# Dilated attention: reload and merge weights emitted four steps later, PSUM banks in three shared pools

## The chip, the cores and the metric

The kernel runs on one core of a Trainium2 chip. Its time is the device time in microseconds, the median of several executions. Beside the times there is a trace of one profiled execution.

## The reference

The kernel computes two transformer blocks on 2048 tokens of width 1024, in float32. The change lies in the first block's dilated attention: 8 heads of 64 columns, and three patterns (window, dilation), which are merged by their softmax denominators:

```python
DIL_PATTERNS = ((128, 1), (512, 4), (2048, 16))
# dilated_branch: query t attends to t + j*dilation, |j| <= window // (2*dilation)
    s = einsum('bnqche,bnkche->bnchqk', qs, kw) * scale + bias   # bias = -slope * distance
    s = where(mask, s, MASK_VALUE)
    m = max(s, axis=-1, keepdims=True); e = exp(s - m); l = sum(e, axis=-1, keepdims=True)
    o = einsum('bnchqk,bnkche->bnqche', e, vw) * (1.0 / l)
    lse = m + log(l)
# dilated_attention
    w = softmax(stack(lses, axis=0), axis=0)
    out = sum(w[..., None] * stack(outs, axis=0), axis=0)
# block
    y = concatenate([a, b], axis=-1) * silu(z);  x = x + y @ w_out
```

## The kernel before

The kernel is one program in six stages, one after the other: projections, differential attention, dilated attention (`phase_b2`, 1321 to about 1709 us of the span), the output product with its gate, and two stages of the second block. Matmuls take their float32 operands as a high and a low part.

`phase_b2` splits the patterns in two. The dense part (names with `n`: d_sn, d_en, d_tn, d_nh, d_nl) is the pattern of dilation 1, with the tokens in their order. The residue part (names with `r` or none: d_sr, d_er, d_tr, d_ph, d_pl) takes the four residue classes mod 4 and holds the patterns of dilation 4 and 16 in one score matrix. Each part has, per head, 16 blocks of 128 queries. For a block, TensorE makes scores into PSUM (L564, L591); VectorE adds the bias and takes the row minimum of the negated scores (L567, L594); ScalarE makes the exponentials with their row sum (L570, L596); TensorE transposes them (L604 into d_tn, L623 into d_tr); they are copied out of PSUM in two parts (dense: ScalarE d_pn, L607, then GpSimd d_nh and d_nl, L611 and L612; residue: ScalarE d_ph, L625, VectorE d_pl, L626); TensorE multiplies them with the values into d_or (L638, L734), four blocks at a time; ScalarE copies that to d_ta (L644), TensorE transposes it back into d_ob (L650), and VectorE sums it into d_o1 or d_o2 (L651).

The dense result of a head (d_o1, with its minimum and sum in two more columns) is in another order of tokens than the residue result (d_o2). So it is stored to DRAM (s_o, L657) and loaded back in the order of the residue classes (d_a, L661, in `load_merge`). Both DMAs are issued on ScalarE's queue; the load waits for the store to land. `load_merge` also loads the gate sz (L665) on SyncE. `weights` (L676) computes the two merge weights: nine small VectorE operations from L686 (d_mm, the first to read d_a) to L696, with two exponentials on ScalarE. The merge itself (scale both results, add, multiply by sz, store to s_y: L702, L719, L720, L673) is on GpSimd and stands in a list `later`, of which one piece is emitted per step (two after the last scores).

The loop goes over steps n: 16 steps are a head, scores of step n are those of the dense blocks n and n + 1 (at even n) and of the residue block n - 3; the other operations follow some steps behind. Counted from a head's first step, its dense result is complete and stored at step 21, `load_merge` is emitted at step 24, `weights` at step 27, the last `back_res` at step 27 too, and the merge's pieces at steps 27 to 35. Head h begins at step 16h. The loads of head h + 1 (q and k, then vn, then vr) are emitted on SyncE at steps 4, 6 and 11 of head h, with the scaled biases of that head (L526, L527) on ScalarE at step 4.

What is emitted is not what each engine runs in order. The program is built with `schedule_with_timeline_sim=True`: a planner with its own model of durations places each instruction on its engine when its inputs and its buffer are free in that model; among instructions that are ready, the one emitted first goes first. The order it makes is fixed in the program, and an engine runs it in that order: an instruction that waits holds up all behind it. The PSUM pools of the stage take eight banks in all, one for a tile; a pool with the same tag for several names hands its banks to whichever comes.

Of the kernel before, what the change touches and what calls it, by code (L numbers as in the profile page):

```python
# [7 lines left out]
F32 = mybir.dt.float32  # L8
# [5 lines left out]
PSUM = bass.MemoryType.PSUM  # L14
DRAM = bass.MemoryType.DRAM

P = 128
# [446 lines left out]
LB = 4  # L464
# [1 line left out]
LEAD = 3  # L466
DN = 2
DR = 2
BACK = 3
WT = 8  # L470


def phase_b2(tc, c, scr, nat_bias, res_bias, res_two):
    nc = tc.nc
    NS = 8 * NT
    with (
# [6 lines left out]
        tc.tile_pool(name="d_h1", bufs=1) as hp1,  # L483
        tc.tile_pool(name="d_p", bufs=2) as pp,
        tc.tile_pool(name="d_o", bufs=2) as op,
        tc.tile_pool(name="d_pon", bufs=1, space=PSUM) as po_n,
        tc.tile_pool(name="d_por", bufs=1, space=PSUM) as po_r,
        tc.tile_pool(name="d_ptr", bufs=2, space=PSUM) as pt_r,
        tc.tile_pool(name="d_psn", bufs=1, space=PSUM) as ps_n,
        tc.tile_pool(name="d_psr", bufs=2, space=PSUM) as ps_r,  # L490
        tc.tile_pool(name="d_ptn", bufs=1, space=PSUM) as pt_n,
    ):
        nb0 = bp.tile([P, 256], F32, name="d_nb0")
        nc.sync.dma_start(nb0, nat_bias)
# [58 lines left out]
        def scores_nat(n):  # L553
            h, t = divmod(n, NT)
            q, k, _, _ = hd[h]
            if t == 0:
                o1s[h] = op1.tile([P, NT, 66], F32, name="d_o1")
                o2s[h] = op.tile([P, NT, 64], F32, name="d_o2", tag="d_o2")
            ml = o1s[h][:, t:t + 2, 64:66]
            ps = ps_n.tile([P, 2, 256], F32, name="d_sn")  # L560
            en = tp.tile([P, 2, 256], F32, name="d_en", bufs=3)
            for u in range(2):
                for i in range(2):
                    nc.tensor.matmul(ps[:, u], q[:, (t + u) * P:(t + u + 1) * P],  # L564
                                     k[i][:, (t + u) * P:(t + u) * P + 256], start=i == 0, stop=i == 1)
            for u in range(2):
                nc.vector.tensor_tensor_reduce(en[:, u], ps[:, u], nb[h % 2], 1.0, 3.0e38, ALU.add, ALU.min,  # L567
                                               ml[:, u, 0:1])
            for u in range(2):
                nc.scalar.activation(en[:, u], en[:, u], AF.Exp, bias=ml[:, u, 0:1], scale=-1.0,  # L570
                                     accum_out=ml[:, u, 1:2])
            en_[n] = en
# [5 lines left out]
        def scores_res(n):  # L578
            h, t = divmod(n, NT)
            q, k, _, _ = hd[h]  # L580
            if t == 0:
                m2s[h] = [sp.tile([P, NT], F32, name=nm, bufs=2) for nm in ("d_m2", "d_l2")]
            g4, s0 = divmod(t, 4)
            cls = 4 * s0 + g4
            m2, l2 = m2s[h][0][:, cls:cls + 1], m2s[h][1][:, cls:cls + 1]
            qr = q.rearrange("p (j r g) -> p j g r", r=P, g=4)[:, s0, g4]
            ps = ps_r.tile([P, 512], F32, name="d_sr")
            lo, hi = span(s0)
            for i in range(2):
                kr = k[i][:, 64:S + 64].rearrange("p (b g u) -> p g b u", g=4, u=16)[:, g4, lo // 16:hi // 16]  # L590
                nc.tensor.matmul(ps[:, lo:hi], qr, kr, start=i == 0, stop=i == 1)  # L591
            er = tp.tile([P, 512], F32, name="d_er")
            off = (3 - s0) * P
            nc.vector.tensor_tensor_reduce(er[:, lo:hi], ps[:, lo:hi], rb[h % 2][:, off + lo:off + hi], 1.0,  # L594
                                           3.0e38, ALU.add, ALU.min, m2)
            nc.scalar.activation(er[:, lo:hi], er[:, lo:hi], AF.Exp, bias=m2, scale=-1.0, accum_out=l2)  # L596
            er_[n] = er

        def trans_nat(n):
            en = en_.pop(n)  # L600
            pt = pt_n.tile([P, 2, 2, P], F32, name="d_tn")
            for u in range(2):
                for j in range(2):
                    nc.tensor.transpose(pt[:, u, j], en[:, u, j * P:(j + 1) * P], c["id"])  # L604
            t = n % 4
            pn = up.tile([P, 2, 2, P], F32, name="d_pn")
            nc.scalar.activation(pn, pt, AF.Copy)  # L607
            if t == 0:
                pn_[n // 4] = [pp.tile([P, 4, 2, P], F32R, name=nm) for nm in ("d_nh", "d_nl")]
            nh, nl = pn_[n // 4]  # L610
            nc.gpsimd.tensor_scalar(nh[:, t:t + 2], pn, 1.0, 1.0, ALU.mult, ALU.mult)  # L611
            nc.gpsimd.tensor_sub(nl[:, t:t + 2], pn, nh[:, t:t + 2].bitcast(F32))  # L612

        def trans_res(n):
            h, t = divmod(n, NT)
            er = er_.pop(n)
            g4, s0 = divmod(t, 4)
            if s0 == 0:
                rpt[h, g4] = (pp.tile([P, 4, 4, P], F32R, name="d_ph"), pp.tile([P, 4, 4, P], F32R, name="d_pl"))
            pt = pt_r.tile([P, 4, P], F32, name="d_tr")  # L620
            ka, kb = [w // P for w in span(s0)]
            for j in range(ka, kb):
                nc.tensor.transpose(pt[:, j], er[:, j * P:(j + 1) * P], c["id"])  # L623
            ph, pl = rpt[h, g4]
            nc.scalar.activation(ph[:, ka:kb, s0], pt[:, ka:kb], AF.Copy)  # L625
            nc.vector.tensor_sub(pl[:, ka:kb, s0], pt[:, ka:kb], ph[:, ka:kb, s0].bitcast(F32))  # L626

        def pv_nat(n):
            h, t = divmod(n, NT)
            nh, nl = [w.rearrange("p t j q -> p (t j) q") for w in pn_.pop(n // 4)]  # L630
            v = hd[h][2]
            po = po_r.tile([P, 512], F32, name="d_or")
            for i in (1, 3, 0, 2, 4):
                lo, hi = max(2 * i - 1, 0), min(2 * i + 1, 8)
                cs = slice(lo // 2 * P, (hi + 1) // 2 * P)
                vi = v[:, t - 3 + i].rearrange("p i d -> p (i d)")
                for x in (nh, nl):
                    nc.tensor.matmul(po[:, cs], vi, x[:, lo:hi].rearrange("p a q -> p (a q)"),  # L638
                                     start=i == 1 and x is nh, stop=i == 4 and x is nl)
            o2s["n"] = evacuate(po)  # L640
# [4 lines left out]
            return ta  # L645

        def back(ta, out):
            pb = po_n.tile([P, 4, 2, 64], F32, name="d_ob")
            for s0 in range(4):
                nc.tensor.transpose(pb[:, s0].rearrange("p i d -> p (i d)"), ta[:, s0 * P:(s0 + 1) * P], c["id"])  # L650
            nc.vector.reduce_sum(out, pb.rearrange("p s i d -> p s d i"), axis=AX.X)  # L651
# [24 lines left out]
        def weights(h):  # L676
# [24 lines left out]
            def scale(x, ap, w):  # L701
                nc.gpsimd.tensor_mul(ap[:, x], ap[:, x], w[:, x].unsqueeze(2).broadcast_to([P, NT // 2, 64]))  # L702

            if h == 7:
                nc.gpsimd.tensor_mul(sd, sz, d2.unsqueeze(2).broadcast_to([P, NT, 64]))
                nc.vector.tensor_mul(av, av, d1.unsqueeze(2).broadcast_to([P, NT, 64]))
                nc.vector.tensor_mul(av, av, sz)

                def tail():
                    nc.vector.tensor_mul(o2, o2, sd)  # L710
                    nc.vector.tensor_add(av, av, o2)
                    store_y(h, av)

                last[h] = [tail]
                return
            soon.extend(lambda x=x: scale(x, av, d1) for x in hs)
            last[h] = [
                *[lambda x=x: scale(x, o2, d2) for x in hs],
                *[lambda x=x: nc.gpsimd.tensor_add(av[:, x], av[:, x], o2[:, x]) for x in hs],  # L719
                *[lambda x=x: nc.gpsimd.tensor_mul(av[:, x], av[:, x], sz[:, x]) for x in hs],  # L720
                lambda: store_y(h, av),
            ]

        def by_group(ap):
            return ap.rearrange("p (j g) d -> p g j d", g=4)

        def pv_res(h, g4, kt):
            if kt == 1:
                hd["por"] = po_r.tile([P, 512], F32, name="d_or")
            po = hd["por"]  # L730
            sa, sb = [w // P for w in span(kt)]
            v = hd[h][3][:, g4 + 4 * kt]
# [4 lines left out]
                o2s["r"] = evacuate(po)  # L737

        def back_res(h, g4):
            back(o2s.pop("r"), by_group(o2s[h])[:, g4])  # L740
            rpt.pop((h, g4))
            if g4 == 3:
                later.extend(soon)
                soon.clear()
                later.extend(last.pop(h))

        later, soon, last = [], [], {}
        for h in range(2):
            load_qk(h)
            load_vn(h)  # L750
# [1 line left out]
        for n in range(NS + LEAD + LB + 12):  # L752
# [12 lines left out]
                back_nat(m - 1)  # L765
            if m % 4 == 3 and 0 <= m < NS:
                pv_nat(m)
            m = n - NT - LN - DN - BACK
            if m % NT == 0 and 0 <= m < NS:
                load_merge(m // NT)  # L770
            m = r - NT - WT
            if m % NT == 0 and 0 <= m < NS:
                weights(m // NT)
            m = r - LB - 4 - DR
            if 0 <= m and m % 4 == 2 and m < NS:
                back_res(m // NT, (m % NT) // 4)
            if 0 <= m < NS and m % 4 < 2:
                for kt in ((1, 2), (0, 3))[m % 4]:
                    pv_res(m // NT, (m % NT) // 4, kt)
            for f in later[:1 if n < NS else 2]:  # L780
                f()
            del later[:1 if n < NS else 2]
# [593 lines left out]
```

## Time and profile before

| | us |
|---|---|
| runs | 2994.63, 3002.65, 3005.74 |
| median | 3002.65 |
| profiled execution | 2997.43 |
| its span, first to last instruction | 2995.7 |
| TensorE busy | 2893.5 |
| mean granted TensorE clock | 0.985 |

A row of a group of waits says which engine and line waited for what, how long in total, how often and the longest. A releaser is inferred: the one that came last. A granted clock of 1.00 is 2.4 GHz, 0.50 is 1.2 GHz. An idle engine costs only where the end waits for it.

### The profile page before, as it was taken

How to read it: one execution, taken by the hardware profiler on the slowest of the kernel's cores; microseconds unless marked ns; L12 is line 12 of the kernel's file. 1: busy time of each engine (PE TensorE's matmuls, PEld its weight loads, DVE VectorE, ACT ScalarE, POOL GpSimd, SP SyncE). 2: the span in 40 equal slices, each digit the busy share in tenths (PEclk: the TensorE clock that was granted, in tenths of full speed). 3: DMA queues.
4: the chain of work that ended last, by engine and by line, in shares of the span. 5: the costliest groups of instructions: out<-in, count | busy, mean ns of one | idle time of the engine just before them, and what ended most of it. 6: DMA issues, size and time to landing. Idle time of an engine off the chain costs nothing. (4 is left out here: it accounts for less than half of the span.)

```text
span 2995.7 us, 45163 instructions
## 1 busy us (share of the span) xinstructions
PE 2893.5 (97%) x15554; PEld 2464.0 (82%) x15554; DVE 1802.1 (60%) x4607; ACT 1563.9 (52%) x3480; POOL 1240.7 (41%) x1156
## 2 busy tenths in 40 slices
PE   9999999999999999988898799999999999999998
PEld 7778888888788888888788678888788888888787
DVE  4115666522788889877666654444535756766765
ACT  5222333311588888878787642222345666666621
POOL 1110111100688888855676610000145565555421
PEclk9999999999999999999899999999999999999999
DMA  6653444414223322148666542332554343332452
GB/s 211 118 155 85 120 114 119 112 65 142 91 55 91 79 64 76 46 111 175 121 147 122 139 149 79 111 96 89 183 162 153 99 133 107 105 113 70 143 192 78
DMA packets 410646, 346.00 MB, mean 115 GB/s; under 512 B 89745, under 2 KB 356401, under 8 KB 408497
## 3 DMA queue, kind: packets, MB, share of 16 engines
q1 hardware_dynamic: 388000, 329.24, 39.3%
q10 hardware_dynamic: 20736, 8.65, 1.6%
q0 software_dynamic: 1680, 5.21, 0.7%
q8 instruction: 124, 2.03, 0.3%
q14 instruction: 106, 0.86, 0.1%
HBM read 227.51 MB, written 116.52 MB: 115 GB/s over the span
## 5 line engine op out<-in xcount | busy, mean ns | idle before, releaser
L190 PE MATMUL psm<-w,hh 128*128 128x512 f32 x1024 | 406.1, 398 | 9.4 <-DVE t L111 7.9
L191 PE MATMUL psm<-w,hl 128*128 128x512 f32 x1024 | 399.9, 392 | 0.0
L192 PE MATMUL psm<-w,hh 128*128 128x512 f32 x1024 | 399.8, 393 | 0.0
L101 POOL TENSOR_TENSOR w<-wraw,w 128x512 fp32r<-128x512 f32 x64 | 81.6, 1295 | 598.9 <-ACT w L100 596.3
L365 POOL TENSOR_TENSOR et<-et 128x1024 f32<-128x1024 f32 x124 | 296.3, 2414 | 0.0
L331 PE MATMUL s_ps<-kst,qst 128*128 128x512 f32 x1024 | 290.5, 408 | 4.1 <-DVE mx L337 3.1
L347 ACT ACTIVATE et<-et,nm 128x2048 f32<-128x2048 f32 x128 | 257.2, 2010 | 5.2
L1027 POOL TENSOR_TENSOR e_wt<-e_raw,e_wt 128x1024 fp32r<-128x1024 f32 x80 | 191.2, 2396 | 112.6 <-ACT e_wt L1026 111.4
L190 PEld LDWEIGHTS psm<-w,hh 128*128 128x128 f32 x1024 | 193.5, 189 | 48.1 <-DVE t L111 8.3
L805 PE MATMUL e_mm<-e_x,e_wt 128*128 128x512 f32 x576 | 228.1, 396 | 1.9 <-DVE e_k L1069 1.7
L807 PE MATMUL e_mm<-e_x,e_wt 128*128 128x512 f32 x576 | 226.8, 394 | 0.0
L192 PEld LDWEIGHTS psm<-w,hh 128*128 128x128 f32 x1024 | 193.2, 189 | 40.8
L806 PE MATMUL e_mm<-e_x,e_wt 128*128 128x512 f32 x576 | 226.6, 393 | 0.0
L191 PEld LDWEIGHTS psm<-w,hl 128*128 128x128 f32 x1024 | 193.7, 189 | 38.2
L331 PEld LDWEIGHTS s_ps<-kst,qst 128*128 128x128 f32 x1024 | 177.0, 191 | 43.7 <-DVE mx L337 17.3
L1128 POOL TENSOR_SCALAR e_es<-e_es,e_l 128x256 f32<-128x256 f32 (+1 forms) x256 | 118.8, 483 | 170.2 <-DVE e_l L1126 101.6
L364 POOL TENSOR_SCALAR et<-et,cc 128x1024 f32<-128x1024 f32 x124 | 138.3, 1132 | 110.4 <-PE psm L192 57.1
L377 DVE TENSOR_TENSOR ptl<-t_ps,pth 128x512 fp32r<-128x512 f32 x256 | 169.3, 684 | 18.9 <-ACT pth L376 18.4
L337 DVE CUSTOM_DVE_ANT_0 et<-s_ps,nd,mx 128x1024 f32<-128x1024 f32 x128 | 163.8, 1280 | 26.8 <-PE s_ps L331 24.9
L1115 DVE CUSTOM_DVE_ANT_0 e_es<-e_s,e_bias,e_sk 128x256 f32<-128x256 f32 (+1 forms) x256 | 117.3, 472 | 103.6 <-PE e_s L1107 72.1
L376 ACT ACTIVATE pth<-t_ps 128x512 fp32r<-128x512 f32 x256 | 143.6, 595 | 42.9 <-PE t_ps L375 38.9
L851 POOL TENSOR_TENSOR c_yn<-c_yn,ssq_sub 128x512 f32<-128x512 f32 x16 | 18.2, 1140 | 355.5 <-DMA c_yn<-s_y 327.5
(268 smaller groups left out, 7866.6 us busy)
## 6 DMA issues: line engine op xcount, KB each, us to landing
e_raw<-in_a_w_in_dram SPq DMA_DIRECT2D x80, 512.0 KB, 3.6
wraw<-in_w_in_dram SPq DMA_DIRECT2D x64, 256.0 KB, 3.5
kst<-s_dk SPq DMA_DIRECT2D x128, 128.0 KB, 3.9
s_xt<-c_at SPq DMA_DIRECT2D x32, 512.0 KB, 6.7
e_x<-s_xt SPq DMA_DIRECT2D x32, 512.0 KB, 7.9
t<-in_x_dram SPq DMA_DIRECT2D x32, 256.0 KB, 5.5
s_dv<-t SPq DMA_DIRECT2D x32, 256.0 KB, 3.0
s_bv<-t SPq DMA_DIRECT2D x32, 256.0 KB, 3.7
```

Of the source, the lines that this page charges most:

```text
L190: nc.tensor.matmul(ps, ah, cur[k][:, 0], start=k == 0, stop=False)
L191: nc.tensor.matmul(ps, al, cur[k][:, 0], start=False, stop=False)
L192: nc.tensor.matmul(ps, ah, cur[k][:, 1], start=False, stop=k == KD - 1)
L331: nc.tensor.matmul(ps[:, b * 512:b * 512 + 512], lhs, heads[h, "k", e, i, 2 * hf + b], start=i == 0, stop=i == 1)
L337: nc.vector.tensor_tensor_reduce(et[:, hf], ps, bias[:, off:off + 1024], 1.0, -3.0e38 if hf == 0 else mx[:, 0:1], ALU.add, ALU.max, mx[:, ...
L347: nc.scalar.activation(ev, ev, AF.Exp, bias=nm, scale=slope, accum_out=st[g]["l"][:, e:e + 1])
L365: nc.gpsimd.tensor_sub(es[0][:, hf], es[0][:, hf], es[1][:, hf])
L377: nc.vector.tensor_sub(tl[:, :, qi], pt, th[:, :, qi].bitcast(F32))
L805: nc.tensor.matmul(ps, ah, bh, start=first, stop=False)
L806: nc.tensor.matmul(ps, al, bh, start=False, stop=False)
L807: nc.tensor.matmul(ps, ah, bl, start=False, stop=last)
L1027: nc.gpsimd.tensor_sub(w[:, 1], raw, w[:, 0].bitcast(F32))
```

## The change

`BACK` goes from 3 to 7 and `WT` from 8 to 12: for the heads 0 to 6 the reload is emitted at step 28 of the head's count and the weights at step 31, behind the step's residue products and not before its `back_res`. For head 7 the reload stays at step 24 of its count and the weights go from 27 to 28. As the weights now come after the last `back_res`, the merge's pieces go straight into `later` (steps 31 to 39); the lists `soon` and `last` are gone. The tile d_o2 is requested at the first `back_res` of a head and not at its first scores. The six PSUM pools (1 bank each for d_ob, d_or, d_sn and d_tn, 2 each for d_tr and d_sr) become three: 2 banks for d_or, 3 for d_tn, d_tr and d_ob together, 3 for d_sn and d_sr together.

```diff
-BACK = 3
-WT = 8
+BACK = 7
+WT = 12
...
-        tc.tile_pool(name="d_pon", bufs=1, space=PSUM) as po_n,
-        tc.tile_pool(name="d_por", bufs=1, space=PSUM) as po_r,
-        tc.tile_pool(name="d_ptr", bufs=2, space=PSUM) as pt_r,
-        tc.tile_pool(name="d_psn", bufs=1, space=PSUM) as ps_n,
-        tc.tile_pool(name="d_psr", bufs=2, space=PSUM) as ps_r,
-        tc.tile_pool(name="d_ptn", bufs=1, space=PSUM) as pt_n,
+        tc.tile_pool(name="d_po", bufs=2, space=PSUM) as po_p,
+        tc.tile_pool(name="d_pt", bufs=3, space=PSUM) as pt_p,
+        tc.tile_pool(name="d_ps", bufs=3, space=PSUM) as ps_p,
...
-                o2s[h] = op.tile([P, NT, 64], F32, name="d_o2", tag="d_o2")
             ml = o1s[h][:, t:t + 2, 64:66]
-            ps = ps_n.tile([P, 2, 256], F32, name="d_sn")
+            ps = ps_p.tile([P, 2, 256], F32, name="d_sn", tag="d_s")
...
-            ps = ps_r.tile([P, 512], F32, name="d_sr")
+            ps = ps_p.tile([P, 512], F32, name="d_sr", tag="d_s")
...
-            pt = pt_n.tile([P, 2, 2, P], F32, name="d_tn")
+            pt = pt_p.tile([P, 2, 2, P], F32, name="d_tn", tag="d_t")
...
-            pt = pt_r.tile([P, 4, P], F32, name="d_tr")
+            pt = pt_p.tile([P, 4, P], F32, name="d_tr", tag="d_t")
...
-            po = po_r.tile([P, 512], F32, name="d_or")
+            po = po_p.tile([P, 512], F32, name="d_or")
...
-            pb = po_n.tile([P, 4, 2, 64], F32, name="d_ob")
+            pb = pt_p.tile([P, 4, 2, 64], F32, name="d_ob", tag="d_t")
...
-                last[h] = [tail]
+                later.append(tail)
                 return
-            soon.extend(lambda x=x: scale(x, av, d1) for x in hs)
-            last[h] = [
+            later.extend([
+                *[lambda x=x: scale(x, av, d1) for x in hs],
                 *[lambda x=x: scale(x, o2, d2) for x in hs],
...
         def back_res(h, g4):
+            if g4 == 0:
+                o2s[h] = op.tile([P, NT, 64], F32, name="d_o2", tag="d_o2")
             back(o2s.pop("r"), by_group(o2s[h])[:, g4])
             rpt.pop((h, g4))
-            if g4 == 3:
-                later.extend(soon)
-                soon.clear()
-                later.extend(last.pop(h))
...
-            m = n - NT - LN - DN - BACK
-            if m % NT == 0 and 0 <= m < NS:
-                load_merge(m // NT)
-            m = r - NT - WT
-            if m % NT == 0 and 0 <= m < NS:
-                weights(m // NT)
+            for h in range(8):
+                at = NT * (h + 1) + LN + DN + (BACK if h < 7 else 3)
+                if n == at:
+                    load_merge(h)
             m = r - LB - 4 - DR
             if 0 <= m and m % 4 == 2 and m < NS:
                 back_res(m // NT, (m % NT) // 4)
             if 0 <= m < NS and m % 4 < 2:
                 for kt in ((1, 2), (0, 3))[m % 4]:
                     pv_res(m // NT, (m % NT) // 4, kt)
+            m = r - NT - (WT if n < NS else LB + DR + 3)
+            if m % NT == 0 and 0 <= m < NS and (n < NS) == (m < NS - NT):
+                weights(m // NT)
```

## Rows read from the trace of the kernel before

**Rows 1.** The page's busy times of the engines: us, share of the span, instructions.

```profile
PE 2893.5 (97%) x15554; PEld 2464.0 (82%) x15554; DVE 1802.1 (60%) x4607; ACT 1563.9 (52%) x3480; POOL 1240.7 (41%) x1156
```

**Rows 2.** Busy time by stretch, heads 0 to 6: us, engines, granted clock, DMA.

```profile
1384.90:1658.60 273.70, 242.28 (x1537) 224.22 (x1536) 185.36 (x588) 215.84 (x608) 191.34 (x219) 0.93 0.63 130
```

**Rows 3.** Busy time by stretch: one between merges; six behind stalls (first two, sum).

```profile
1460.00:1480.00 20.00, 20.00 (x135) 18.83 (x134) 15.54 (x47) 18.49 (x53) 19.67 (x26) 1.00 0.73 171
...
1391.10:1394.50 3.40, 3.40 (x14) 3.06 (x14) 1.13 (x5) 0.33 (x1) 0.77 (x1) 0.50 0.12 13
1445.70:1455.90 10.20, 6.05 (x27) 5.68 (x28) 5.04 (x17) 6.48 (x20) 1.88 (x2) 0.50 0.20 61
...
sum 40.90, PE 28.62 PEld 25.90 DVE 18.33 ACT 28.74 POOL 15.87; mean PE 4.77 PEld 4.32 DVE 3.05 ACT 4.79 POOL 2.65
```

**Rows 4.** Waits of TensorE, 1384.9 to 1660 us: total us, times, longest.

```profile
PE d_sn L564 <- DVE d_o L567: 11.0, 3, 4.1
PE d_tn L604 <- ACT d_pn L607: 10.8, 4, 4.0
PE d_tr L623 <- DVE d_pl L626: 3.6, 4, 2.9
PE d_sr L591 <- DVE d_m L594: 2.2, 6, 0.5
PE d_or L638 <- POOL d_nl L612: 1.2, 2, 1.0
```

**Rows 5.** Waits of all engines, 1300 to 1715 us, for d_a and for s_o.

```profile
DVE d_mm L686 <- DMA d_a<-s_o: 36.4, 8, 8.4
...
ACT d_er L596 <- DMA s_o<-d_o: 11.2, 2, 5.7
...
ACT d_pn L607 <- DMA s_o<-d_o: 9.2, 2, 5.1
```

**Rows 6.** Timeline of ScalarE at head 1's reload: start, us, instruction [idle before].

```profile
1443.18 0.37 ACTq L661 DMA_DIRECT2D d_a<-s_o  x1
1443.60 0.60 ACT L625 ACTIVATE d_ph<-d_tr 128x512 fp32r<-128x512 f32 x1 [5.49 <-DMA s_o<-d_o]
...
1445.44 0.41 ACT L526 ACTIVATE d_nb__13769<-d_nb 128x256 f32<-128x256 f32 x1
```

**Rows 7.** Instructions of a line up to 1364.4, 1445.4, 1582 us; SyncE at 1364.

```profile
L564 PE MATMUL d_sn<-d_k,d_q x40: 278/283/570, 1321.0 to 1361.9; 128*128 128x256 f32 x40
...
1364.45 8.24 SPq L665 DMA_DIRECT2D d_sz<-s_sz  x8
...
L625 ACT ACTIVATE d_ph<-d_tr x36: 471/538/621, 1346.6 to 1444.6; 128x384 fp32r<-128x384 f32 x18, 128x512 fp32r<-128x512 f32 x18
...
L596 ACT ACTIVATE d_er<-d_er,d_m x90: 601/674/740, 1334.6 to 1575.9; 128x384 f32<-128x384 f32 x45, 128x512 f32<-128x512 f32 x45
```

**Rows 8.** Landing: all stores L657; SyncE at 1440; reloads L661, heads 1 and 2.

```profile
DMA to landing us min/median/max: 5.9/10.1/11.2
...
1440.27 2.54 SPq L549 DMA_DIRECT2D d_vr<-s_bv  x4
...
DMA to landing us min/median/max: 5.9/5.9/5.9
...
DMA to landing us min/median/max: 3.7/3.7/3.7
```

**Rows 9.** Timelines of TensorE and, last row, ScalarE between two merges.

```profile
1408.27 0.60 PE L604 MATMUL d_tn<-id,d_en 128*128 128x128 f32 x4
...
1410.55 0.60 PE L650 MATMUL d_ob<-id,d_ta 128*128 128x128 f32 x4
...
1411.95 0.60 PE L604 MATMUL d_tn<-id,d_en 128*128 128x128 f32 x4
...
1408.99 0.60 ACT L607 ACTIVATE d_pn<-d_tn 128x512 f32<-128x512 f32 x1 [0.34 <-PE d_tn L604]
```

**Rows 10.** Timeline of TensorE at the stage's end.

```profile
1708.52 0.80 PE L805 MATMUL c_mm<-c_wo,c_at 128*128 128x512 f32 x1 [0.78 <-DVE d_o L651]
```

More of the change, by code (lines that the diff above doesn't have):

```diff
@@ L721, in weights @@
                 lambda: store_y(h, av),
-            ]
+            ])
         def by_group(ap):
@@ L728, in pv_res @@
             if kt == 1:
-                hd["por"] = po_r.tile([P, 512], F32, name="d_or")
+                hd["por"] = po_p.tile([P, 512], F32, name="d_or")
             po = hd["por"]
@@ L739, in back_res @@
         def back_res(h, g4):
+            if g4 == 0:
+                o2s[h] = op.tile([P, NT, 64], F32, name="d_o2", tag="d_o2")
             back(o2s.pop("r"), by_group(o2s[h])[:, g4])
             rpt.pop((h, g4))
-            if g4 == 3:
-                later.extend(soon)
-                soon.clear()
-                later.extend(last.pop(h))
-        later, soon, last = [], [], {}
+        later = []
         for h in range(2):
```

## The prediction, made before the result was known

> **What bounds the kernel now.** I read the page's busy times first, then the table of stretches for the dilated stage, then who waited for whom, and last the timelines around one merge. TensorE is busy 97% of the span [rows 1], so only TensorE's idle time, or time at its lower clock, can be won. Of the dilated stage the reader should look at the stretch from the first store of a dense result (head 0) to the seventh (head 6), 1384.9 to 1658.6 us: TensorE works 242.28 of 273.70 us, so it idles 31.4 us, and its mean granted clock is 0.93 [rows 2]. Between two merges it has no idle time at all: 20.00 of 20.00 us at full clock, with 135 matmuls [rows 3]. A head has 256 matmuls here (the 2048 of the stage over 8 heads), so undisturbed it takes 256/135 x 20 = 37.9 us; the six heads of the stretch take 273.7/6 = 45.6. The 7.7 us between them is what is there to win per head, and all of it lies around the merge.
>
> The waits say how. TensorE's own long waits are for d_sn's bank (11.0 us, three times), for d_tn's bank (10.8 us, four times) and for d_tr's (3.6 us) [rows 4]. Those banks were late because VectorE and ScalarE stood still: ScalarE waited 11.2 + 9.2 = 20.4 us in four heads for the store s_o of a dense result to land, as the reload d_a is issued on ScalarE's queue and has to wait for that store, and VectorE waited 36.4 us, eight times, at the first instruction of the weights (d_mm, L686) for d_a [rows 5]. In head 1 the two follow each other: ScalarE idles 5.49 us before the reload goes out at 1443.18, and all that stands behind it on ScalarE (exponentials, evacuations) waits with it [rows 6]; then d_a needs 5.9 us to land [rows 8] while VectorE stands before d_mm, with the score reductions queued behind it. The clock follows: in six stretches, 40.90 us together, it is 0.50, which is the lower level of 1.2 GHz, each at or just behind a stall; TensorE is busy 28.62 us of them [rows 3]. At 2.4 GHz the same matmuls take about half, so the lower clock costs about 14 us. The whole price of the merges is the waits for d_sn and d_tn plus the 2.9 us at d_tr in head 1, some 24.7 us, and this 14: 39 us.
>
> **The change part by part.**
>
> *Reload and weights four steps later.* Nothing is removed or added: the same reload, the same nine small VectorE operations and two exponentials per head, only emitted at steps 28 and 31 of a head's count in place of 24 and 27 (weights now behind the step's result products). At 45.6/16 = 2.85 us per step that would be 11.4 us, more than the 10.1 us (median) that the store takes to land [rows 8], so if instructions stood on their engines in the order in which they are emitted, ScalarE's wait would be gone; d_mm would still follow its load by three steps, 8.6 us (7.1 at 37.9 us per head), which covers a landing of 3.7 or 5.9 us. But they don't stand in that order. The planner fills each engine with what is ready in its own model of time. On SyncE all eight sz loads of heads 0 and 1 go out from 1364.45 on, when 40 score matmuls (scores of steps 0 to 18) had been issued; head 1's are emitted at step 40 [rows 7]. On ScalarE the scaled bias of head 4 (L526), emitted at step 52, runs at 1445.44 right behind the 36th copy of L625, which belongs to step 42 [rows 6, 7]: ten steps early, at once when its buffer was free. So ScalarE has free slots in the plan, and what is ready isn't held back by its late place. The reload already stands where it became ready there and not at its step: head 4's, emitted at step 88, has 90 exponentials L596 before it, the last of step 92 [rows 7]. Emitted at step 92 it can give way only to instructions of steps 88 to 92 that are ready at that moment. Reading ScalarE's order behind the reload in each of the heads 0 to 6, I find 0 to 3 of these, about one of 0.6 us on the mean (an L625 copy took 0.60 [rows 6]). The same holds for d_mm on VectorE, behind which the next instructions belong to later steps still. So I cost the move at -0.6 us for each of 7 heads, -4 us. Its ends are -39 us (all of the merges' price) and 0. I take the end next to zero, as it is the placing that the rows show.
>
> *The merge's GpSimd work* (nine pieces, L702 to L720 and the stores) moves with the weights: from steps 27 to 35 to 31 to 39. It needs the weights, so it starts as early as now, but gives way sooner to the copies d_nh and d_nl that TensorE needs. TensorE's wait for d_nl is 1.2 us in the stretch [rows 4]; ends -1 and 0, I take 0. In SyncE's queue the sz loads now stand behind d_vr and not before, but already go out when their buffer frees; their data are used last in the merge: 0. The o2 tile is requested later, which frees a buffer that no row shows anyone waiting for: 0. Head 7's reload stays at its step and its weights go from step 139 to 140, with the final stretch's TensorE work beside it: 0.
>
> *Banks.* Scores had 1 + 2 banks and have 3; per two steps they take three tiles, so each tile still follows the one three before it: 0. Results get a second bank, and no wait of TensorE for a result bank is among its waits: 0 in the stretch. In the tail the next stage's first product waits 0.78 us for d_ob's bank [rows 10], which now can be one of the result banks, free earlier; the waits there for d_tr's two banks get a third. Ends -4 and 0, I take -2. Transposes and d_ob had 2 + 1 + 1 banks and have 3 for four tiles per two steps, and this is the part that can cost. At the undisturbed pace d_tn is written at 1408.27, copied out from 1408.99 for 0.60 us, and written again at 1411.95, so its bank is free for 2.36 us before it is needed; if d_ob (1410.55) takes the same bank, the spare time is 0.96 us [rows 9]. In a ScalarE stall TensorE then stops up to 1.4 us sooner: 7 stalls x 1.4 = 10 us at the upper end, 0 at the lower (where it would have stopped at d_tr first, as in head 1). I take +3, as in four of seven waits it was d_tn that stopped it, and TensorE's order puts d_ob ahead only in part of these.
>
> Sum: -4 + 0 - 2 + 3 = -3 us. The profiled execution took 2997.43 us (its span 2995.7 and 1.7 around it), which is 5.2 under the median of 3002.65; 2997.4 - 3 + 5.2 = 2999.6. I forecast 2999 us, no change that can be told: half a per cent, 15 us, is about what a measurement of this kernel can tell from none.
>
> **Rivals.**
>
> *The moves take effect* (the plan is crowded there after all, or the new banks crowd it). For it speaks that the two waits are the largest of the stage and that 11.4 us would cover the store; against it the early placing in rows 7. It would give back up to the 39 us: 2997.4 - 39 + 5.2 = 2964. One thing speaks against its full size: the reload would then go out after d_vr. In head 1 it went out within 3 us of four d_vr loads (1440.27) and took 5.9 us to land, in head 2, without these, 3.7 [rows 8]; 2.2 us more per head, which three steps still cover. The Trainium skill's page "DMA: Bandwidth & Descriptors" (Issuing engines are not separate DMA queues) says the same of any two queues: transfers issued by different engines share the same 16 DMA engines and interleave, so ScalarE's queue is no protection from SyncE's loads. By that rule all seven reloads would land in about 5.9 us; the trace agrees in head 1, and the time of this rival stays.
>
> *Slower: the shared transpose banks bind in every step.* Place: TensorE before d_ob or d_tn, also between merges. It decides from where the copy out of the bank ends later than the 0.96 us that are spare; ScalarE has 18.5 of 20 us of work at that pace [rows 3], so a copy that queues behind two others of 0.6 us is already too late. Price: the present bank waits of this kind (d_sr) are 2.2 us in 6, 0.37 each [rows 4]; once in each of the 64 pairs of steps that is 24 us: 2997.4 + 24 + 5.2 = 3027. Against it: at the pace of rows 9 the copies came in time.
>
> *The stalls shorten a little and the clock stays up.* If the 0.6 us and the tail come as I say and the clock falls in none of the merges, the 14 us come back too: 2997.4 - 4 - 14 + 5.2 = 2985. For it speaks that behind head 0's store the clock fell for 3.4 us only, in head 1 for 10.2 [rows 3]; against it that a stall of about 4 us stays in most heads.
>
> **How the numbers follow.** Forecast (no change) 0.47, the moves take effect 0.22, the clock stays up 0.12, banks bind 0.19. The forecast's own range comes from its ends without the large -39: 2985 to 3013. The 80% range reaches from 2960, just under the first rival, to 3022, where the unknown bank cost is most of its price; what is left out is the upper half of the slower rival and a gain beyond all the merges. Faster by over 0.5% (under 2987.6): 0.22 + most of 0.12 + little of the forecast = 0.33. Slower (over 3017.7): most of 0.19 and a little of the forecast, 0.21. Same: 0.46.
>
> **What would show it.** Right: in the profile after, VectorE's wait at d_mm for d_a stays near 36 us and ScalarE's for s_o over 20, and the reload follows the store on ScalarE by as many instructions as now. Wrong in favour of the first rival: both waits under 10 us, the six lower-clock stretches gone, the head period near 38 us. Wrong in favour of the second: d_ob or d_tn waiting for the copies of d_pn, d_pl or d_o in dozens of short pieces, the undisturbed 20.00 of 20.00 gone. If d_or or d_sr head TensorE's waits, my count of the other banks was wrong.

## The result, and the profile after

The changed kernel takes 3032.1 us (median of 4 runs, 3026.38 to 3041.27) against 3002.55 in the same session: ratio 1.0105, 95% interval 1.0073 to 1.0137. The forecast was 2999, the range ended at 3022. The profiled execution took 3026.38 us, 28.95 more than before. The page's busy times, then the stage by stretch (to the first store of a dense result, to the seventh, to the last sum of d_ob, and a stretch between merges; columns as in [rows 2]):

```profile
PE 2898.3 (96%) x15554; PEld 2468.7 (82%) x15554; DVE 1801.8 (60%) x4607; ACT 1565.2 (52%) x3480; POOL 1238.6 (41%) x1156
```
```profile
1319.10:1391.20 72.10, 58.24 (x361) 53.79 (x359) 45.77 (x149) 52.91 (x158) 28.27 (x33) 0.91 1.00 197
1391.20:1683.90 292.70, 246.74 (x1542) 227.78 (x1542) 182.13 (x584) 214.24 (x599) 186.51 (x213) 0.92 0.62 120
1683.90:1734.60 50.70, 37.71 (x223) 32.38 (x221) 30.43 (x75) 30.74 (x76) 29.61 (x29) 0.93 0.43 107
1460.00:1480.00 20.00, 20.00 (x132) 18.77 (x131) 15.08 (x48) 17.98 (x50) 18.88 (x22) 1.00 0.60 147
```

TensorE's total hardly changed [rows 1]; it idles. The kernel before, in the same three parts:

```profile
1320.40:1384.90 64.50, 56.08 (x362) 52.18 (x361) 44.09 (x151) 51.04 (x153) 23.92 (x28) 0.95 1.06 214
...
1658.60:1708.50 49.90, 37.99 (x231) 32.91 (x229) 29.91 (x69) 30.61 (x74) 31.40 (x30) 0.93 0.47 123
```

The stage grew by 7.6 + 19.0 + 0.8 = 27.4 us, with the middle part of before in [rows 2]. In that part TensorE idles 45.96 us (31.42 before), and its work takes 4.5 us longer. The stretches at half clock, 1.2 GHz, are 47.6 us against 40.9, and TensorE is busy 33.77 us of them against 28.62 [rows 3]; if the same matmuls take half as long at 2.4 GHz, that makes about 2.6 of the 4.5 us. Their sum, then:

```profile
sum 47.60, PE 33.77 PEld 31.43 DVE 27.15 ACT 31.07 POOL 14.15; mean PE 4.22 PEld 3.93 DVE 3.39 ACT 3.88 POOL 1.77
```

In the stretch between merges TensorE has still no idle time [rows 3]. Who waited for whom in the middle part (engine, what for; us in total, times, longest):

```profile
PE d_ob L646 <- DVE d_pl L622: 19.6, 4, 5.8
PE d_ob L646 <- ACT d_ta L640: 6.7, 10, 0.9
PE d_tr L619 <- ACT d_pn L603: 5.2, 2, 4.7
PE d_or L634 <- POOL d_nl L608: 3.8, 3, 1.7
PE d_sr L587 <- DVE d_o L563: 3.5, 1, 3.5
PE d_tn L600 <- DVE d_o L647: 3.0, 1, 3.0
PE d_sn L560 <- DVE d_m L590: 2.3, 5, 1.6
PE d_tn L600 <- DVE d_pl L622: 1.5, 3, 0.6
```

The sum of such waits is 45.6 us against 30.8 (the 28.8 of [rows 4] and two rows of 1.0 us, one of them d_ob's). d_ob now heads the list with 26.3 us, and the waits for d_sn and d_tn that headed it before have gone from 21.8 to 6.8 us: TensorE stops at another place, and for longer. The merges' own waits are still there (stage, all engines):

```profile
DVE d_mm L682 <- DMA d_a<-s_o: 27.8, 7, 7.2
...
ACT d_ph L621 <- DMA d_vn<-s_bv: 13.6, 2, 6.9
ACT d_ph L621 <- DMA s_o<-d_o: 11.9, 2, 7.0
...
ACT d_er L592 <- DMA s_o<-d_o: 6.1, 1, 6.1
```

The row with d_vn, heads 3 and 5, is a wait for the store too, as the times show, and only put down to another load. Head 3's store went out at 1538.15 and took 10.7 us to land, head 5's at 1637.00 and 10.7 us, and the reloads on ScalarE went out just behind, at 1549.08 and 1647.89:

```profile
1549.08 0.37 ACTq L657 DMA_DIRECT2D d_a<-s_o  x1
1549.49 0.60 ACT L621 ACTIVATE d_ph<-d_tr 128x512 fp32r<-128x512 f32 x1 [6.94 <-DMA d_vn<-s_bv]
```

So ScalarE stood 31.6 us at the reloads of heads 1 to 5, where it had stood 25.9 (the 20.4 of [rows 5] and head 1's 5.5 of [rows 6]).

One merge shows how they meet. ScalarE's timeline at head 2's reload:

```profile
1487.67 0.44 ACTq L653 DMA_DIRECT2D s_o<-d_o  x1
1488.23 0.60 ACT L603 ACTIVATE d_pn<-d_tn 128x512 f32<-128x512 f32 x1 [0.47 <-ACT d_ph L621]
...
1491.26 0.72 ACT L592 ACTIVATE d_er<-d_er,d_m 128x512 f32<-128x512 f32 x1
...
1498.68 0.37 ACTq L657 DMA_DIRECT2D d_a<-s_o  x1
1499.10 0.60 ACT L621 ACTIVATE d_ph<-d_tr 128x512 fp32r<-128x512 f32 x1 [7.02 <-DMA s_o<-d_o]
```

then VectorE's and TensorE's:

```profile
1499.72 0.69 DVE L622 TENSOR_TENSOR d_pl<-d_tr,d_ph 128x512 fp32r<-128x512 f32 x1 [6.69 <-ACT d_ph L621]
```
```profile
1500.56 1.09 PE L646 MATMUL d_ob<-id,d_ta 128*128 128x128 f32 x4 [5.80 <-DVE d_pl L622]
```

The reload stands eight places behind its store, seven operations between, as it did before in this head, and waits 7.02 us (5.69 before). d_ph and with it d_pl come late, the d_tr tile keeps its bank, and d_ob, which now takes its bank from the same three, stops TensorE for 5.80 us. The largest wait of the first part is new: 6.93 us at d_or for d_nh. GpSimd copies the next head's keys to the other 64 partitions first (d_k), and stood 9.15 us for their load.

```profile
1380.52 0.58 PE L634 MATMUL d_or<-d_nh,d_vn 128*128 128x256 f32 x1 [6.93 <-POOL d_nh L607]
```
```profile
1376.71 2.35 POOL L532 TENSOR_SCALAR d_k<-d_k 64x512 fp32r<-64x512 f32 x4 [9.15 <-DMA d_k<-s_bk]
...
1379.84 0.62 POOL L607 TENSOR_SCALAR d_nh<-d_pn 128x512 fp32r<-128x512 f32 x1
```

GpSimd stood there before, too, but TensorE's order did not have it wait (its longest wait for GpSimd in the stage was 2.5 us):

```profile
1378.72 2.36 POOL L535 TENSOR_SCALAR d_k<-d_k 64x512 fp32r<-64x512 f32 x4 [6.36 <-DMA d_k<-s_bk]
...
1381.87 0.62 POOL L611 TENSOR_SCALAR d_nh<-d_pn 128x512 fp32r<-128x512 f32 x1
```

### The profile page after: what moved, and what is told of

Read it like the earlier page. It is cut to its first block, busy times and chain, and to the rows that moved or that the text cites. A ratio compares the mean times of both kernels' runs of the same rounds, so it can differ in the third digit from the quotient of the medians.

```text
span 3024.1 us, 45103 instructions
## 1 busy us (share of the span) xinstructions
PE 2898.3 (96%) x15554; PEld 2468.7 (82%) x15554; DVE 1801.8 (60%) x4607; ACT 1565.2 (52%) x3480; POOL 1238.6 (41%) x1156
## 4 chain that ended last, share of the span: by engine, by line
PE 82%; DMA 7%; ACT 3%; DVE 3%; POOL 2%; issue 1%; SPq 1%; ACTq 0%; DVEq 0%; POOLq 0%
PE s_ps L331 7%; PE psm L190 7%; PE psm L192 7%; PE psm L191 7%; PE e_mm L800 5%; PE e_mm L802 5%; PE e_mm L801 5%; PE c_mm L800 4%; PE c_mm L801 4%; PE c_mm L802 4%; PE t_ps L375 3%; DMA s_o<-d_o 2%; PE o_ps L389 2%; PE o_ps L391 2%; PE o_ps L390 2%; PE f_mm L801 2%
## 5 line engine op out<-in xcount | busy, mean ns | idle before, releaser
L337 DVE CUSTOM_DVE_ANT_0 et<-s_ps,nd 128x1024 f32<-128x1024 f32 x128 | 156.1, 1220 | 14.4 <-PE s_ps L331 7.0
```

Source lines behind the costliest of these rows:

```text
L337: nc.vector.tensor_tensor_reduce(et[:, hf], ps, bias[:, off:off + 1024], 1.0, -3.0e38 if hf == 0 else mx[:, 0:1], ALU.add, ALU.max, mx[:, ...
```

## The experiments

All ratios are to the kernel before, on the same chip, with 95% intervals.

**The two halves.** e1_moves: the changed code with the pool lines (and tile calls) of before. e2_banks: the kernel before with the pool lines of the change.

> The changed kernel with the six separate bank pools of before: the moves alone. Banks theory: the moves place nothing anew (the reload stands 8 instructions behind its store in either kernel) and the 30 us come with the shared banks, so 3000 us, 2990 to 3012; TensorE's waits as before, d_ob in none of them. Moves theory: GpSimd's merge pieces and the weights at their new steps cost it, so 3025 to 3035, with waits for d_nl as in the changed kernel.

> The kernel before with the three shared bank pools alone, without the moves. Banks theory: 3032 us, 3022 to 3042, with TensorE waiting for d_pl and for d_ta ahead of d_ob, some 26 us of it between the first store and the seventh. Moves theory: 3003 us. If both parts are needed together (interaction): between, 3010 to 3020.

Measured: 0.9998 (0.9986 to 1.0010), 3006 us, and 1.0116 (1.0098 to 1.0135), 3042 us. The banks are all of it. e1's program has TensorE's, GpSimd's and SyncE's instructions in exactly the order of before, and in ScalarE's and VectorE's a few are moved by some places; e2's differs from the changed kernel's by the place of one VectorE instruction. So the pools alone set the new order.

**The banks one kind at a time**, in the kernel before (e3 in the changed one).

```diff
 e7_scores_shared: -d_psn bufs=1, d_psr bufs=2    +d_ps bufs=3
 e8_trans_shared:  -d_ptn bufs=1, d_ptr bufs=2    +d_pt bufs=3 (d_tn, d_tr)
 g1_ring_four:     -d_ptn 1, d_ptr 2, d_pon 1     +d_pt bufs=4 (d_tn, d_tr, d_ob)
 e3_ob_alone:      -d_po bufs=2                   +d_po bufs=1, d_pb bufs=1 (d_ob)
```

> The changed kernel with the dense and residue outputs' transposes (d_ob) taken out of the three shared banks into a bank of their own, results in one bank as before; scores and probabilities' transposes still share three each. If d_ob in the shared ring is what costs (19.6 us of waits for d_pl and 6.7 us for d_ta in the changed kernel, all at d_ob), these 26 us go: 3006 us, 2998 to 3014. If the sharing of the scores' banks or of the probabilities' transposes costs it, it stays near 3030.

> The kernel before with one edit: dense and residue scores share three banks instead of one and two. With d_ob in its own bank the shared kernel was still 12 us over before, 6.8 of them one wait for d_nh. If the scores' sharing does that: 3014 to 3020, with this wait in the trace; if the transposes' does: 3000 to 3010.

> The kernel before with one edit: the two kinds of probabilities' transposes (d_tn, d_tr) share three banks instead of one and two, d_ob in its own. If these make the 12 us: 3014 to 3020; if the scores' sharing does: 3000 to 3010.

> The kernel before with d_tn, d_tr and d_ob in one ring of four banks, one bank for the results, scores' banks as before: the same number of transposes' banks, only in common. If d_ob's turn in the ring costs (it waits for d_pl in each merge stall: 19.6 to 23.8 us in the kernels with three): 3022 to 3035. If the bank given to the results does: 3007 to 3018, as with d_tn and d_tr alone in the ring.

Measured: e3 1.0039 (1.0025 to 1.0053), 3018 us, above its range; e7 1.0000 (0.9991 to 1.0008); e8 1.0035 (1.0022 to 1.0047); g1 1.0082 (1.0068 to 1.0096), 3032 us. So the scores' banks cost nothing, d_tn and d_tr in one ring 0.35%, d_ob in that ring 0.47% more although no bank is lost, and the bank given from it to the results the last 0.3% (1.0082 to 1.0116; the intervals just miss each other). One view shows d_ob's part: its transposes, in the stage, and what TensorE idled for before them (us, times), in the kernel before,

```profile
L650 PE MATMUL d_ob<-id,d_ta x256: 269/273/477, 1352.0 to 1707.5; 128*128 128x128 f32 x128
its engine sat idle before it (us, times) until:
  ACT d_ta L644: 4.5, 5
```

the changed one,

```profile
its engine sat idle before it (us, times) until:
  DVE d_pl L622: 19.6, 4
  ACT d_ta L640: 8.9, 13
```

g1,

```profile
its engine sat idle before it (us, times) until:
  ACT d_ta L642: 23.4, 24
```

and e3, where d_ob has its own bank again:

```profile
its engine sat idle before it (us, times) until:
  ACT d_ta L641: 2.8, 4
```

**The moves made real.** e4 ties the reload and d_mm to a later instruction of their engines (`issue_after`: issue order only): the reload behind the exponential of the head's residue step 29, d_mm behind the reduction of step 33. e6 does so for d_mm alone; e10 is e6 with the reload issued by SyncE. All have six pools, and a third buffer for the residue part's minimum and sum (d_m2, d_l2). Head 7's reload, and d_mm of the last two heads, are not tied.

```diff
-BACK = 7; WT = 12
+BACK = 11; WT = 17        # e4; e6 and e10: 7 and 17
+with tc.issue_after(last_exp):          # e4 only
     nc.scalar.dma_start(a1, s_o[h])     # e10: nc.sync
+with tc.issue_after(last_reduction):
     nc.vector.tensor_tensor(mm, m1, m2, ALU.min)
```

> The six pools of before and the moves of the change, but the dense reload is now bound in ScalarE's order behind the exponential of the third residue step of the next head but one step group (some 38 instructions behind its store instead of 8), and d_mm in VectorE's order behind the score reduction five steps later. The rival of the prediction that the moves take effect: the d_mm wait (36.4 us in 8) and ScalarE's waits for the store (some 20 us) go, and with them 15 to 39 us: 2964 to 2988. The theory that these waits are hidden anyway, or turn into others: 2995 to 3008.

> Of the held kernel only the weights' half: d_mm bound behind the score reduction of the second half head, the reload again 8 instructions behind its store on ScalarE, six separate pools. If VectorE's wait at d_mm (36.4 us in 8) was what the gain of 46 us came from: 2965 to 2980. If ScalarE's wait at the reload for the store (some 20 us) holds TensorE as long by itself: 2985 to 3005.

> The kernel with d_mm alone held (3002 us), the reload issued from SyncE's queue instead of ScalarE's; six pools. If what d_mm's stall left behind was ScalarE standing at the reload until the store had landed (33.6 us in 6 in that kernel), it goes without binding the reload to any place: 2960 to 2972, as with both held. If the reload on SyncE holds up the loads of the next head's keys instead: 2980 to 3005, with TensorE waiting for d_k or d_vr.

Measured: e4 0.9848 (0.9829 to 0.9867), 2961.2 us; e6 0.9981 (0.9968 to 0.9994), 3002 us; e10 0.9894 (0.9880 to 0.9907), 2974 us, between its two ranges. e4 beats both kernels; in its program the reloads of heads 0 to 6 stand 37 to 42 places behind their stores (8 to 12 before, 8 to 10 in the changed kernel). Its middle part and its end:

```profile
1389.40:1621.60 232.20, 226.27 (x1524) 211.91 (x1523) 187.11 (x576) 209.98 (x599) 180.65 (x208) 0.99 0.74 149
1621.60:1663.00 41.40, 34.49 (x222) 31.57 (x221) 33.71 (x79) 31.08 (x80) 35.21 (x34) 0.96 0.50 135
```

TensorE is busy 97% of the part and a head takes 38.7 us, where I had reckoned 37.9 without disturbance. In e6 VectorE's wait at d_mm is all but gone (0.7 us), but ScalarE stands at the reload as before (29.6 us in six heads in the kernel before), and TensorE now waits behind it at d_ob:

```profile
ACT d_ta L644 <- DMA s_o<-d_o: 33.6, 6, 6.7
...
PE d_ob L650 <- ACT d_ta L644: 27.8, 11, 5.0
```

e10 takes this wait off ScalarE: its middle part is e4's, its end is not (PE idle for d_pl 14.1 us there; why d_pl is late was not followed up).

```profile
1389.00:1620.30 231.30, 226.63 (x1537) 213.81 (x1537) 187.88 (x580) 210.79 (x599) 181.44 (x210) 0.99 0.75 150
1620.30:1676.90 56.60, 40.07 (x222) 35.28 (x221) 41.38 (x79) 31.63 (x80) 41.06 (x41) 0.82 0.41 108
```

**Shared banks where no stall is left**, all on e4: e5 has the three pools; h1 and f1 what e7 and e8 have; e9 and e11 are e5 with

```diff
 e9_held_four:      d_po bufs=1, d_pt bufs=4
 e11_held_ob_three: d_pt bufs=2 (d_tn, d_tr), d_pb bufs=1 (d_ob)
 e12_back_later:    back_nat(m - 1) at m % 4 == 0 -> back_nat(m - 2) at m % 4 == 1
 f2_held_or2 (on e4): d_por bufs=2, d_ptr bufs=1
```

> The held reload and weights (2961 us with six separate pools) now with the three shared pools of the change. If sharing costs through the merge stalls alone (d_pl late behind d_mm, and d_ob behind d_pl: 19.6 to 23.8 us in four pieces), there is no stall to lengthen, and it stays within 10 us: 2961 to 2972, the rest being the one wait of 6.9 us for d_nh at the start of the stage. If the shared banks cost in every step, the whole 30 us come back: 2985 to 2995.

> The held kernel with six pools (2961 us), the scores' three banks in common, all else as there. If the common scores' banks let the scores run further ahead of the transposes and cost where no merge stall is left: 2975 to 2990. If the transposes' ring with d_ob is all of it: 2958 to 2966.

> The held kernel with six pools (2961 us), d_tn and d_tr in one ring of three banks, all else as there. If the common ring of the two is a cost of its own, as in the kernel before (10 us): 2968 to 2980. If the second result bank is what costs: 2958 to 2966.

> The held kernel with shared banks (2991 us), but four banks for the three kinds of transposes (d_tn, d_tr, d_ob in one ring) and one for the results: as many transposes' banks as the six pools have. If it is the lost bank that costs the 27 us over the held kernel with six pools (2961): 2961 to 2970. If it is the common ring, which makes tiles of three kinds take their banks in one order: 2980 to 2992.

> The held kernel with shared banks, but d_ob in a bank of its own and d_tn with d_tr sharing two: three transposes' banks in all and two for the results, as in the change. If the number of banks is what costs: 2985 to 3000. If d_ob in the ring of the others costs: 2961 to 2972.

> The held kernel with shared banks (2991 us), the dense results' transpose d_ob written one step later, so that d_ta is ready when its turn in the ring comes. TensorE waits there 7.5 us for d_ta (10 pieces) and 12.0 us for d_nh between the first store and the seventh. If the place of d_ob in the ring's order is the cost: 2975 to 2985, the waits for d_ta gone. If the count of banks is: 2988 to 2995, the same idle time under another name.

> The held kernel with six pools, two banks for the results and one for d_tr: every kind in its own banks, three transposes' banks as in the change, no common ring. If the second result bank pulls the dense result matmuls ahead of their operands: 2978 to 2995, with TensorE waiting for d_nh and d_nl. If the common ring is what costs: 2961 to 2972.

Measured: e5 0.9937 (0.9923 to 0.9950), h1 0.9850 (0.9835 to 0.9865), f1 0.9862 (0.9847 to 0.9877), e9 0.9929 (0.9915 to 0.9942), e11 0.9943 (0.9930 to 0.9955), e12 0.9920 (0.9907 to 0.9933), f2 1.0232 (1.0218 to 1.0246). The same 240 us (1400 to 1640) of e4, f1, e9, e11, e5, one after the other; the count after TensorE's busy time is its matmuls:

```profile
1400.00:1640.00 240.00, 235.96 (x1597) 221.59 (x1596) 198.05 (x603) 219.17 (x624) 189.31 (x215) 1.00 0.71 148
```
```profile
1400.00:1640.00 240.00, 235.26 (x1599) 222.11 (x1598) 191.56 (x607) 220.87 (x626) 189.91 (x217) 1.00 0.76 148
```
```profile
1400.00:1640.00 240.00, 222.43 (x1478) 209.10 (x1478) 177.52 (x554) 203.43 (x576) 172.47 (x198) 0.99 0.70 142
```
```profile
1400.00:1640.00 240.00, 230.40 (x1524) 213.79 (x1523) 190.85 (x580) 212.88 (x597) 179.97 (x206) 0.99 0.72 142
```
```profile
1400.00:1640.00 240.00, 220.34 (x1458) 207.35 (x1457) 175.70 (x547) 202.57 (x565) 169.66 (x196) 0.98 0.71 140
```

My theory that the banks cost only through the merge stalls fell with e5: no stall is left, and 27 us come back. h1 (1597 matmuls) and f1 lose nothing in this stretch; f1's 2967 us in all lie just between its two ranges. With d_ob in the ring it is 1478, even with four banks. But d_ob is not all: with d_ob apart and two banks for d_tn and d_tr (e11), 1524. f2, without any ring, lost 116 us on e4, outside both of its ranges; that its one bank for d_tr is the reason is likely but not shown. e12's 2983 us lie in the range for d_ob's place, but its interval overlaps e5's, and the waits for d_ta are not gone: TensorE idles 8.3 us for it at d_ob, 12.4 in e5.

The ring also changes where the planner puts d_ob. In the programs of before and of e4, d_ob follows the last product of its own result with no matmul between in 3 cases of 64; in the changed kernel and e2 in 8, in g1, e5 and e9 in 11. There ScalarE still has to make d_ta when TensorE arrives.

**The place of the result products.** Behind the last d_tn of four steps the dense d_or started 7 to 12 us later (median, start to start) in the kernels with one result bank, 1.2 us in the changed kernel, e2 and e5. There it meets GpSimd's copies: TensorE's longest wait in e5 is 20.2 us, in six pieces, at d_or for d_nh. f3 (on the changed kernel) and f4 (on e5) tie the dense products behind the step's d_tr transposes:

```diff
+with tc.issue_after(last_d_tr_transpose):
     for i in (1, 3, 0, 2, 4): ... nc.tensor.matmul(po[:, cs], vi, x, ...)
```

> The changed kernel (3032 us) with one binding added: the dense result matmuls are queued on TensorE behind the residue transposes written in their step, three or four of these behind the last d_tn of the group, as they stood before. If their early place behind d_tn is what costs: 3005 to 3018, with the waits for d_nh and d_nl (13 us) and for d_ta (7 us) gone. If the ring's turn is: 3027 to 3037, the time lost at another wait.

> The held kernel with shared banks (2991 us) and the same binding of the dense result matmuls. If their early place is what costs there too: 2965 to 2978, TensorE waiting for neither d_nh nor d_ta in the stretch (19.5 us before). If the ring's turn is: 2986 to 2996.

Measured: f3 1.0127 (1.0114 to 1.0141), 3046 us; f4 0.9931 (0.9919 to 0.9943), 2986 us. The early place was undone (8.4 and 6.8 us), in f4 the waits at the dense d_or for GpSimd fell from 20.2 to 5.4 us, and yet f4's time can't be told from e5's and f3's is above both of its ranges, so this theory fell too. In f3 the merges' stalls grew: from the first store on there are five waits at d_mm of 7.3 to 8.8 us, where the changed kernel had 27.8 us in seven over the whole stage:

```profile
DVE d_mm L683 <- DMA d_a<-s_o: 41.7, 5, 8.8
```

## Why the prediction was wrong

**The moves: right.** I costed the reload and the weights at -4 us, as the planner places what is ready and not what is late in the text. e1 says 0, in the old order of instructions. Of the signs I named, the distance to the store held, and so did ScalarE's wait for s_o, which even grew (31.6 us in heads 1 to 5). VectorE's wait at d_mm stayed near 36 us in e1 (38.8) but fell to 27.8 in the changed kernel: in head 3, for one, it had waited 8.4 us there and now stands 7.2 us at d_pl, behind the stopped ScalarE, and then only 2.2 us at d_mm. The rival that the moves take effect was priced at 39 us under the profiled run; e4, which moves both further and ties them, came out 36.4 under it (2961.07 against 2997.43). In its middle part the idle time fell by 25.5 us and the busy time by 16.0, where I had 24.7 for the waits and 14 for the clock. Its premise was wrong for this change, its price near. The slower landing beside d_vr hardly came up: in e4 head 1's reload went out at 1452.4, over 10 us behind d_vr (1438.8), and the reloads landed in 3.6 to 4.9 us, not 5.9; in the changed kernel those of heads 0 to 6 landed in 4.5 to 6.9.

**The step that failed is the term of the transposes' banks: +3, with +10 as its upper end.** It measured 29 us in the changed kernel and 35 in e2, which has the banks alone (1.0116). I priced a loss of spare time, 1.4 us for each of 7 stalls, in TensorE's order of before [rows 9]. But the pools are an input of the planner, and the order came out anew. Four things were not in my term: d_ob, which had nothing to wait for but its own operand, waited 28.5 us in the changed kernel (4.5 before), four times behind d_pl in a merge and 13 times for d_ta just made, while those at d_sn and d_tn fell by 15 us; ScalarE stood 5.7 us longer at the reloads; TensorE came to d_or while GpSimd still stood before the key copies, 6.9 us; and the clock was low for 47.6 us where it was 40.9. The 80% range ended at 3022, at most of the slower rival's 24 us; the loss lies above that price too.

**The slower rival** (banks bind, 3027) came nearest to the time, and d_ob was its place. But its price, 24 us, was near the 29 by luck, as its form was wrong: not dozens of short pieces in every step, as the 20.00 of 20.00 us between merges remained, but 14 waits in the middle part, of which four make 19.6 us. In the kernels without stalls it was nearer the mark: there e9 and e5 lose 7 to 9% of the matmuls in the same 240 us, and a head takes 41.6 and 42.0 us against e4's 38.7. A spare time of 0.96 us, read from the old order in one stretch between merges, was no proof that the ring is wide enough in the new one.

**The rest.** Scores' banks at 0: right (e7, h1). The second result bank at 0 and -2 in the tail: the tail grew by 0.8 us, and moving one bank from the transposes to the results changes e9's 0.9929 to e5's 0.9937, which can't be told apart. The clock as a term of its own, 14 us: in e4 3.4 us of half clock are left in the middle part, and TensorE's busy time there is 16.0 us shorter. The forecast's own range, 2985 to 3013: its upper end is the banks' +10, but my terms' lower ends (-4, -1, -4) add up to 2994 only; 2985 was the third rival's time.

**Open.** Whether the time goes because a tile's bank in the ring is taken or because the planner writes another order for a ring was not separated. Both occur: the four waits for d_pl (19.6 us in the changed kernel, 23.8 in e2) are for a bank that another tile still holds, while in g1 all of d_ob's 23.4 us are for its own operand. Nor was it shown why two banks for d_tn and d_tr cost as much in e11 as d_ob in the ring.

## What to carry to other kernels

Where a planner orders the work by readiness, moving a line can move nothing, as here; before pricing such a move, look at where the instruction stood, and tie it to another one if it is to move (here from about 9 places behind the store to about 40, and 1.5%). Banks shared among tiles of several kinds change two things: a tile that waited for its operand alone can now wait for another kind's slow reader (19.6 us here), and the planner may write another order, in which it comes too early for its own operand (23.4 us in g1). So don't price the sharing by the spare time at an even pace in the old order; look at the new one. When two engines wait in a row, one for a store and one for the reload behind it, taking away one wait alone may gain little (e6, 0.2%) where taking away both gains much (e4, 1.5%).
